# The last 512 value columns of layer 2 as one group, and a last tile closed by column halves, in an fp32 encoder trunk on one core

## The chip, the cores and the metric

The kernel runs on one core of one Trainium2 chip (trn2). The metric is the device time of one execution in microseconds, from runs of the same program; the median of them counts. One execution was also taken by the hardware profiler; the rows quoted in this document come from such executions. Engines are called as in the profile: PE is TensorE with its matmuls, PEld its weight loads, DVE is VectorE, ACT ScalarE, POOL GpSimd and SP SyncE, which issues all DMAs here.

## The reference

The reference is one inference step of a two-layer encoder for 1024 prompt rows and 8 x 16 sample rows, model width 1024, 16 heads of 64 in layer 2, feed-forward width 2816. Layer 1 mixes with sliding-window attention (mixer A); layer 2 with a band of chunks (mixer B), whose keys and values are projected once from the residual stream after layer 1, with a scale and shift of their own. Every sub-layer is closed by

    x <- LN(alpha * x + (1 + gate) * f(x * (1 + scale) + shift))

with LN(x) = (x - mean) * rsqrt(var + 1e-5) * g + b. Cut to what the change touches:

```python
v = (hkv @ w_kv_b[:, 1024:])            # values of layer 2: 1152 rows x 1024 columns
k = (hkv @ w_kv_b[:, :1024])            # keys
q = hm @ w_q_b[0]                       # queries, from hm = x*(1+scale)+shift
s = q k^T * scale + bias, banded; p = softmax(s); o = p v   # each of 16 heads
...
u = causal conv of (h @ w_up); f = (gelu(g) * a) @ w_down   # feed-forward
y = LN(alpha * x + (1 + gate) * f)      # the output, 1152 x 1024
```

All of it is fp32. The kernel's outputs are y, the keys and values and the convolution's state rows.

## The kernel before

The 1152 rows are nine tiles of 128; tile 8 holds the sample rows. Each fp32 operand of a large product is split into a high part (a cast to fp32r) and a low part (the rest, also fp32r), and a product is made of three: low x high, high x low, high x high. So a tile of 128 rows times 1024 rows of weight is 3 x 8 = 24 matmuls into one PSUM bank, whatever the number of columns, up to 512. `wload` (L178) brings a block of weights: a DMA into one of two staging buffers `ws`, a cast on ACT (L165) for `wh`, a subtraction (L176) on POOL or DVE for `wl`. The results go to one of four weight slots, `wslots`, or a place that is given.

The order of each engine's instructions is set by a scheduler that runs over the program in the order it is written, with estimated times; `issue_after` holds some steps back behind others.

The stages of layer 2's mixer, in the order of the program (`attention`, called with l = 1):

- The first quarter of the values, `vproj` (L430): for each token tile in the order 0, 1, 2, 8, 3, 4, 5, 6, 7, `mmX` (L387, matmul L395) multiplies the tile's activations, which lie in `H` (called HX in the trace), by 256 columns; ACT casts the high part from PSUM (L444), DVE subtracts for the low part (L445), and both go out as one DMA to vH (L446). Tiles 4 to 8 are also copied (L450) and stored as outputs.
- Eight chunks of 128 key columns, `kproj` (matmul L383, 384 tokens at a time, three blocks a chunk), with `rescale` on POOL between them.
- The other three quarters of the values, 256 columns each, with two weight slices (512 rows x 256 columns, 24 matmuls a tile together) in slots that rotate.
- Then the slot ring is set to the first two slots, and `qload(0)` loads the first chunk of query weights into slot 0, which the last quarter of the values has used too.
- `load_hm` (L897): for each of the nine tiles a DMA of the residual stream into one of three buffers F (L903), a scale and shift by eight ACT instructions (L907, one for each 128 columns; on DVE at L1006 and L1007 for tile 8), and a split into H: cast (L165) and low part (L176, DVE). A tile of H can be written only when the value projection has read it for the last time.
- Then the attention, head after head: `qblock` (matmuls L383, 24 a block of 384 tokens; drains on ACT at L579 and L590, on DVE at L591), scores (L633 and L636), softmax (DVE L599, ACT L603 with the exponential), transposes (L659), values (L678), sums and normalisation. The projection of the next head's queries is put between the steps of the present one to keep PE full.

At the end of the program stands `down_phase` of layer 2, the feed-forward's second product. Tiles go in groups of three; the last group's last 7 inner steps (the tail) are run tile by tile. `mm` (L1372) makes, for each inner step, three matmuls for each of the two halves of 512 output columns, in two banks. `drain` multiplies by the gate (L1390), `finish` adds the residual and sums (L1401), and `norm_last` (L948) does the LayerNorm: mean (L951), square on ACT (L954), variance (L955), `rsqrt` (L929 to L934). For the very last tile, 8, L961 to L964 then follow each other on DVE, ACT, POOL and DVE, and L965 stores the 128 x 1024 tile.

## Time and profile before

| what | value |
|---|---|
| median of 3 runs | 2803.09 us |
| lowest and highest | 2794.26 and 2809.61 us |
| profiled execution, its own time | 2800.65 us |
| its span, first to last instruction | 2798.5 us |
| mean granted clock of TensorE | 0.988 |
| busy share of the span: PE, PEld | 96%, 86% |
| busy share of the span: DVE, ACT, POOL | 60%, 50%, 38% |
| memory traffic over the span | 165 GB/s |

The own time of the profiled execution lies 2.15 us above its span and 2.44 us below the median. A row of the timeline gives the start, the duration, the engine, the line, the operation, out <- in and the count; what stands in brackets is how long the engine had been idle before it and what it waited for. A row of groups gives the count, then the busy time and the mean nanoseconds of one, then the idle time in front. A row of the chain gives when a piece of the chain that ended last began and how long it held it. Durations of matmuls overlap, since they are pipelined: how far apart two starts are is a better price than a row's duration.

### The profile page before, as it was taken

To read this page: it belongs to the slowest core of one execution; us is meant where nothing else is said; L and a number is where in the kernel's file an instruction comes from. 1 tells how busy PE (TensorE), PEld (TensorE's weight loads), DVE (VectorE), ACT (ScalarE), POOL (GpSimd) and SP (SyncE) were. 2 spreads that over 40 slices of the span, in tenths; PEclk is the share of its full clock that TensorE was granted. 3 is DMA by queue.
4 is the path that set the end of the run, shared out by engine and by line. 5 is a ranking of instruction groups with operands and counts; after the bars stand their busy time and mean duration, and the time that the engine had idled before them with its cause. 6 is when DMAs were issued, how large, how long until landed. Compare 5 with 4: busy or idle time off the path is not lost.

```text
span 2798.5 us, 48858 instructions
## 1 busy us (share of the span) xinstructions
PE 2700.2 (96%) x18086; PEld 2415.9 (86%) x18086; DVE 1665.2 (60%) x3830; ACT 1408.9 (50%) x3012; POOL 1056.7 (38%) x1086
## 2 busy tenths in 40 slices
PE   8999889999999999999999999989899999999998
PEld 5887768999999998888999888867799999998886
DVE  4465757765555566766212677775966555567774
ACT  3465744544444444545425666662555445555441
POOL 1122337676566630001541121141877666640000
PEclk9999999999999999999999999999999999999999
DMA  9655443244444457865975456684222222238661
GB/s 331 193 155 164 124 140 113 97 139 138 155 134 128 146 158 266 310 215 182 303 249 177 113 150 185 168 250 132 99 89 74 78 83 75 76 104 290 232 209 71
DMA packets 215870, 454.47 MB, mean 162 GB/s; under 512 B 39280, under 2 KB 115264, under 8 KB 215632
## 3 DMA queue, kind: packets, MB, share of 16 engines
q1 hardware_dynamic: 215632, 451.35, 50.1%
q8 instruction: 143, 2.34, 0.3%
q14 instruction: 95, 0.78, 0.1%
HBM read 359.40 MB, written 101.30 MB: 165 GB/s over the span
## 4 chain that ended last, share of the span: by engine, by line
PE 77%; DVE 8%; DMA 7%; issue 4%; ACT 3%; POOL 1%; SPq 1%; POOLq 0%; ACTq 0%; DVEq 0%
PE PS L1225 34%; PE PS L1376 17%; PE PS L383 9%; PE PS L395 7%; DMA F<-in_adaw_dram 3%; PE PS L678 2%; PE PS L318 2%; PE PS L659 2%; PE PS L633 1%; DMA ws<-in_wo_dram 1%; DVE F L599 1%; PE PS L636 1%; DVE x1att L176 1%; PE PS L977 1%; PE PS L799 1%
## 5 line engine op out<-in xcount | busy, mean ns | idle before, releaser
L176 POOL TENSOR_TENSOR wl<-ws,wh 128x512 fp32r<-128x512 f32 (+1 forms) x217 | 324.2, 1497 | 649.3 <-ACT wh L165 628.3
L1279 DVE SCALAR_TENSOR_TENSOR PS<-F,PS 128x512 f32<-128x512 f32 (+2 forms) x704 | 349.1, 516 | 143.5 <-ACT PS L1286 63.6
L165 ACT CAST wh<-ws 128x512 fp32r<-128x512 f32 (+1 forms) x321 | 245.2, 769 | 313.6 <-PE PS L1376 99.3
L1225 PE MATMUL PS<-HX,wh 128*128 128x288 f32 x2616 | 401.0, 297 | 0.0
L1225 PEld LDWEIGHTS PS<-HX,wh 128*128 128x128 f32 x2616 | 364.4, 189 | 8.2 <-issue 8.2
L1376 PE MATMUL PS<-wh,HX 128*128 128x512 f32 x1164 | 361.7, 389 | 0.8 <-DVE HX L176 0.8
L1376 PEld LDWEIGHTS PS<-wh,HX 128*128 128x128 f32 x1164 | 218.4, 188 | 46.1 <-DVE HX L176 1.3
L1225 PE MATMUL PS<-HX,wl 128*128 128x288 f32 x1536 | 254.6, 297 | 0.2 <-ACT F L1254 0.2
L383 PE MATMUL PS<-HX,wh 128*128 128x384 f32 x1248 | 245.9, 340 | 0.0
L1376 PE MATMUL PS<-wl,HX 128*128 128x512 f32 x582 | 226.7, 390 | 0.6 <-DVE wl L176 0.6
L1225 PEld LDWEIGHTS PS<-HX,wl 128*128 128x128 f32 x1536 | 220.5, 189 | 7.1 <-issue 5.8
L383 PEld LDWEIGHTS PS<-HX,wh 128*128 128x128 f32 x1248 | 217.3, 189 | 5.4 <-issue 3.1
L1225 PE MATMUL PS<-x1att,wh 128*128 128x288 f32 x1168 | 181.9, 298 | 2.9 <-DVE x1att L176 1.3
L1286 ACT ACTIVATE PS<-F 128x512 f32<-128x512 f32 x176 | 138.1, 785 | 76.3 <-DVE F L1258 64.9
L1225 PEld LDWEIGHTS PS<-x1att,wh 128*128 128x128 f32 x1168 | 163.9, 189 | 8.9 <-issue 4.9
L395 PE MATMUL PS<-wh,HX 128*128 128x256 f32 (+1 forms) x936 | 168.4, 310 | 0.8 <-DVE C L599 0.8
L165 ACT CAST HX<-F 128x384 fp32r<-128x384 f32 (+3 forms) x232 | 136.6, 605 | 62.7 <-PE PS L1376 10.2
L717 POOL TENSOR_TENSOR F<-F,gatt 64x512 f32<-64x512 f32 x62 | 79.5, 1282 | 234.8 <-DVE F L690 181.5
L176 DVE TENSOR_TENSOR HX<-F,HX 128x384 fp32r<-128x384 f32 (+2 forms) x188 | 133.3, 719 | 37.2 <-ACT HX L165 33.6
L1376 PE MATMUL PS<-HX 128*128 128x512 f32 x630 | 145.1, 389 | 0.0
L395 PEld LDWEIGHTS PS<-wh,HX 128*128 128x128 f32 x936 | 133.8, 191 | 10.3 <-issue 1.5
L383 PE MATMUL PS<-HX,wl 128*128 128x384 f32 x624 | 130.3, 348 | 10.1 <-DVE HX L167 4.8
(244 smaller groups left out, 5486.2 us busy)
## 6 DMA issues: line engine op xcount, KB each, us to landing
F<-in_adaw_dram SPq DMA_DIRECT2D x112, 512.0 KB
ws<-in_wup_dram SPq DMA_DIRECT2D x92, 512.0 KB
ws<-in_wdn_dram SPq DMA_DIRECT2D x88, 512.0 KB
actD<-F SPq DMA_DIRECT2D x44, 576.0 KB
F<-actD SPq DMA_DIRECT2D x132, 192.0 KB
F<-in_wdn_dram SPq DMA_DIRECT2D x44, 512.0 KB
x1att<-kH SPq DMA_DIRECT2D x60, 256.0 KB
xd<-F SPq DMA_DIRECT2D x27, 512.0 KB
```

The costliest lines, as they stand in the source:

```text
L165: self.lastact = nc.scalar.copy(out, in_).ins
L176: self.eng(el).tensor_sub(lo, src, hi.bitcast(F32))
L318: mm = nc.tensor.matmul(ps[32 * j : 32 * j + 32, hf * 256 : hf * 256 + 256], self.cT[:, k * 32 : k * 32 + 32], w[n][:, j * 256 : j * 256 + ...
L383: self.nc.tensor.matmul(out, w[a][:, k * 128 : k * 128 + 128], self.Hx(p, k, s0, n), start=i == 0, stop=i == 23)
L395: self.nc.tensor.matmul(out[:, 0:n], H[:, t0 // 128, p, j * kn + k, :], w[a][:, k * n : k * n + n], start=i == 0, stop=i == 23,)
L659: nc.tensor.transpose(t[:, m * 128 : m * 128 + 128], p[:, (kt - k0) * 128 : (kt - k0) * 128 + 128], self.ident)
L678: nc.tensor.matmul(ob[:, i0 * 128 : i0 * 128 + w], vst[a][:, kt, :], pp[:, m1 : m1 + w], start=cnt == 0, stop=cnt == 2 * len(order) - 1, s ...
L717: self.eng("v" if last else "p").tensor_mul(on[r, q], on[r, q], rb[r, :])
L1225: nc.tensor.matmul(out, w[f][a][:, k * 128 : k * 128 + 128], x[:, k, :], start=start and i == 0, stop=i == 11, skip_group_check=True,)
L1279: nc.vector.scalar_tensor_tensor(o, v, w(i), o, op0=ALU.mult, op1=ALU.add)
L1286: nc.scalar.activation(yp, u[:, bl, 2:258], AF.Identity, bias=w(3), scale=w(2))
L1376: nc.tensor.matmul(ps, h[p][:, i * 128 : i * 128 + 128], w[q][:, hf * 512 : hf * 512 + 512], start=j == 0 and k == 0, stop=j == NFF - 1 an ...
```

## The change

It has two parts. The first is in layer 2's value projection. `vproj` takes its weights, the first column and the number of columns as arguments. The second quarter is still 256 columns, but its weights are placed in the buffers of the attention's first head (X1), which are free there. The last two quarters become one group of 512 columns: 24 matmuls of 128 x 512 for each tile, with four weight slices (256 rows x 512 columns) that lie partly in X1 and partly in the last two slots. Its drains have three buffers of their own, and each cast, subtraction, copy and store has 512 columns. Slots 0 and 1 are then not used by the last group, which the ring of query weights takes over.

The second part is `close`, called in place of `mm`, `drain`, `finish` and `norm_last` for the last tile of the output. It runs the 21 tail matmuls of the left 512 columns, then those of the right; each half has its multiplication by the gate (L957 after) and its sum (L958). Then come the mean (L968), the square on ACT (L969), beside it (x + s) * g on DVE (L970), the variance and rsqrt, and for each half x * r + b on DVE (L974) with a store of its own (L975).

The line numbers of the changed kernel lie two higher in the middle of the program: L633 before is L635 after, L907 is L909; in `vproj` L444 is L445 and L450 is L449.

PE's order before, from the end of the value groups to the first scores; L395 is the value projection, L383 the query projection, wl and wh the low and high parts of a weight, `x1att` the buffer of the attention:

```order
L395 MATMUL PS<-wh,HX 128x256 x4
L383 MATMUL PS<-HX,wl 128x384 [waits Pool_49]
L383 MATMUL PS<-HX,wl 128x384 x7
L383 MATMUL PS<-HX,wh 128x384 [waits Activation_49]
L383 MATMUL PS<-HX,wh 128x384 x15
L383 MATMUL PS<-HX,wl 128x384 [waits DVE_49,Activation_49]
L383 MATMUL PS<-HX,wl 128x384 x7
L383 MATMUL PS<-HX,wh 128x384 [waits DVE_49]
L383 MATMUL PS<-HX,wh 128x384 x15
L633 MATMUL PS<-x1att_12291 128x128 [waits DMAHW4_49,DMAHW3_49,DVE_49]
```

After, at the same place:

```order
L395 MATMUL PS<-wh,HX 128x512 x2
L383 MATMUL PS<-HX,wl 128x384 [waits Activation_49]
L383 MATMUL PS<-HX,wl 128x384 x7
L383 MATMUL PS<-HX,wh 128x384 x16
L383 MATMUL PS<-HX,wl 128x384 [waits Activation_49]
L383 MATMUL PS<-HX,wl 128x384 x7
L383 MATMUL PS<-HX,wh 128x384 x16
L383 MATMUL PS<-HX,wl 128x384 [waits Activation_49]
L383 MATMUL PS<-HX,wl 128x384 x7
L383 MATMUL PS<-HX,wh 128x384 [waits DVE_49]
L383 MATMUL PS<-HX,wh 128x384 x15
L635 MATMUL PS<-x1att_12291 128x128 [waits DMAHW7_49,DMAHW0_49,DVE_49]
```

Before, two blocks of queries, 48 products, stand there ahead of the first score; after, three blocks, 72 products; the first of them waits for ACT and no longer for POOL.

ACT's order after, in the first part of the last value group; L445 casts a value tile out of PSUM, L909 scales a tile of hm, and L165 with HX<-F is the cast of a tile of hm into H:

```order
L445 CAST HX<-PS 128x8x64 [waits DMAHW0_49,DMAHW5_49,PE_49,Activation_49]
L165 CAST HX<-F 128x1024
L445 CAST HX<-PS 128x8x64 [waits PE_49]
L165 CAST HX<-F 128x1024
L909 ACTIVATE F<-F,C 128x128 [waits DMAHW0_49,DVE_49]
L909 ACTIVATE F<-F,C 128x128 x7
L445 CAST HX<-PS 128x8x64 [waits DMAHW1_49,PE_49]
L165 CAST HX<-F 128x1024
L909 ACTIVATE F<-F,C 128x128 [waits DMAHW2_49,DVE_49]
L909 ACTIVATE F<-F,C 128x128 x7
L449 COPY F<-PS 128x512 [waits DMAHW6_49,PE_49]
```

The value casts and the refill of H alternate as they did in the last quarter before, now with 512 columns to a cast; the casts of the first two chunks of query weights stand ahead of these rows, where before the first of them stood behind the last value cast.

DVE's last rows after, in the last tile (`x1dn` is the tile's row, C a column of small numbers, ISA the row that multiplies or adds and sums):

```order
L957 TENSOR_TENSOR x1dn_23884<-PS,x1dn_23884 128x512 [waits PE_49]
L958 ISA x1dn_23884,C<-x1dn_23884 128x512 [waits DVE_49]
L958 ISA C 128x1
L968 TENSOR_SCALAR C<-C 128x1 [waits DVE_49]
L970 SCALAR_TENSOR_TENSOR x1dn_23884<-x1dn_23884,C,F 128x1024 [waits DVE_49]
L971 TENSOR_SCALAR C<-C 128x1 [waits Activation_49]
L932 RECIPROCAL C<-C 128x1 [waits Activation_49]
L934 TENSOR_SCALAR C<-C 128x1 [waits DVE_49]
L935 TENSOR_SCALAR C<-C 128x1 [waits DVE_49]
L936 TENSOR_TENSOR C<-C 128x1 [waits DVE_49]
L974 SCALAR_TENSOR_TENSOR x1dn_23884<-x1dn_23884,C,F 128x512 [waits DVE_49]
L974 SCALAR_TENSOR_TENSOR x1dn_23884<-x1dn_23884,C,F 128x512
```

The left half's pair L957 and L958 stands earlier in DVE's queue, between the last small steps of tile 7. Before, two L1390, one L1401 of 1024 columns, the same small steps, L961 and L964 with its wait for POOL stood here.

The diff:

```diff
--- before.py
+++ after.py
@@ -427,27 +427,26 @@
             if n > m:
                 nc.sync.dma_start(self.kS[l][rows, :], t[:, m:n])
 
-    def vproj(self, l, q, banks, tmp):
+    def vproj(self, l, src, c0, n, banks, tmp, dst=None):
         nc = self.nc
-        w = [self.wload(self.I[("wv0", "wv1")[l]][q, i], el="pv"[l == 0]) for i in range(2)]
+        kn = 1024 // n
+        w = [self.wload(src[i], el="vp"[l], dst=dst and dst[i]) for i in range(8 // kn)]
         o0 = (896, 512)[l]
-        cs = slice(q * 256, q * 256 + 256)
+        cs, hs = slice(c0, c0 + n), slice(c0 // 64, (c0 + n) // 64)
         for t in LV:
             ps = self.bank(banks.next())
-            self.mmX(ps, t * 128, w, 4, 256)
+            self.mmX(ps, t * 128, w, kn, n)
             hl, v = tmp.next()
-            v = v[:, 0:256]
+            hl, v = hl[:, 0 : 2 * n], v[:, 0:n]
             ts = slice(t * 128, t * 128 + 128)
             if t < 8:
-                h4 = hl[:, 0:512].rearrange("p (h i d) -> p h i d", i=2, d=64)
-                p3 = ps[:, 0:256].rearrange("p (h d) -> p h d", d=64)
+                h4 = hl.rearrange("p (h i d) -> p h i d", i=2, d=64)
+                p3 = ps[:, 0:n].rearrange("p (h d) -> p h d", d=64)
                 nc.scalar.copy(h4[:, :, 0, :], p3)
                 nc.vector.tensor_sub(h4[:, :, 1, :], p3, h4[:, :, 0, :].bitcast(F32))
-                nc.sync.dma_start(
-                    self.vH[l][ts, 4 * q : 4 * q + 4, :], hl[:, 0:512].bitcast(F32).rearrange("p (h d) -> p h d", d=128)
-                )
+                nc.sync.dma_start(self.vH[l][ts, hs, :], hl.bitcast(F32).rearrange("p (h d) -> p h d", d=128))
             if t * 128 >= o0:
-                nc.scalar.copy(v, ps[:, 0:256])
+                nc.scalar.copy(v, ps[:, 0:n])
                 nc.sync.dma_start(self.O[("va", "vb")[l]][t * 128 - o0 : t * 128 - o0 + 128, cs], v)
             if t == 8:
                 nc.sync.dma_start(self.vS[l][:, cs], v)
@@ -524,7 +523,7 @@
         with ExitStack() as es:
             if l == 0:
                 es.enter_context(self.tc.issue_after(self.lastx))
-            self.vproj(l, 0, kvb, kvt)
+            self.vproj(l, I[("wv0", "wv1")[l]][0], 0, 256, kvb, kvt)
         if l == 0:
             self.skew(0)
         else:
@@ -533,8 +532,11 @@
                 self.kproj(1, c, self.wload(I["wk1"][c]), kvb, kvt)
                 self.rescale(c, zr)
             self.rescale(8, zr)
-            for q in range(1, 4):
-                self.vproj(1, q, kvb, kvt)
+            vt = [(self.X2[:, i * 1024 : i * 1024 + 1024], self.F[:, i * 512 : i * 512 + 512]) for i in range(3)]
+            spare = [tuple(self.X1[:, o + i : o + i + 1024] for i in (0, 1024)) for o in (0, 2048, 5120, 7168)]
+            spare += [self.wslots[2], (self.wslots[3][0], self.X1[:, 4096:5120])]
+            self.vproj(1, I["wv1"][1], 256, 256, kvb, kvt, spare[0:2])
+            self.vproj(1, I["wv1h"], 512, 512, kvb, Ring(vt), spare[2:6])
             self.wring = Ring(self.wslots[0:2])
             qload(0)
             self.load_hm(Ring([pall[:, i * 1024 : i * 1024 + 1024] for i in range(3)]), self.affine(4, (8, 9), 1))
@@ -944,6 +946,33 @@
         nc.vector.tensor_scalar_add(v, mv[:, 1:2], EPS)
         self.rsqrt(r, v)
         return mv[:, 0:1], r
+
+    def close(self, t, row, x, ydst, product, junk):
+        nc = self.nc
+        part, rr = self.sm.next(), self.sm.next()
+        s, v, r = part[:, 0:1], rr[:, 0:1], rr[:, 1:2]
+        halves = [slice(hf * 512, hf * 512 + 512) for hf in range(2)]
+        for hf, n in enumerate(halves):
+            ps = product(hf)
+            nc.vector.tensor_mul(row[:, n], ps, self.gateS[:, n])
+            nc.vector.tensor_tensor_reduce(
+                out=row[:, n],
+                in0=row[:, n],
+                in1=x[:, n],
+                scale=1.0,
+                scalar=0.0,
+                op0=ALU.add,
+                op1=ALU.add,
+                accum_out=part[:, hf : hf + 1],
+            )
+        nc.vector.tensor_scalar(s, s, part[:, 1:2], -1.0 / D, op0=ALU.add, op1=ALU.mult)
+        nc.scalar.activation(junk, row, AF.Square, bias=s, accum_out=v)
+        nc.vector.scalar_tensor_tensor(x, row, s, self.lng, op0=ALU.add, op1=ALU.mult)
+        nc.vector.tensor_scalar(v, v, 1.0 / D, EPS, op0=ALU.mult, op1=ALU.add)
+        self.rsqrt(r, v)
+        for n in halves:
+            nc.vector.scalar_tensor_tensor(x[:, n], x[:, n], r, self.lnb[:, n], op0=ALU.mult, op1=ALU.add)
+            nc.sync.dma_start(ydst[t * 128 : t * 128 + 128, n], x[:, n])
 
     def norm_last(self, t, x, s, ydst, junk):
 
@@ -1369,8 +1398,8 @@
         todo = []
         aff = None
 
-        def mm(w, h, t, i, j):
-            for hf in range(2):
+        def mm(w, h, t, i, j, hs=(0, 1)):
+            for hf in hs:
                 ps = self.bank(2 * i + hf)
                 for k, (p, q) in enumerate(((1, 0), (0, 1), (0, 0))):
                     nc.tensor.matmul(
@@ -1452,9 +1481,18 @@
                     finish(*todo.pop(0))
             wh = [load(g, j) for j in range(NFF - nt, NFF)]
             for i, t in enumerate(ts):
+                row = rows.next()
+                if last and final and i == 2:
+
+                    def product(hf):
+                        for k, (w, h) in enumerate(wh):
+                            mm(w, h, t, i, NFF - nt + k, (hf,))
+                        return self.bank(2 * i + hf)
+
+                    self.close(t, row, xs[i], xdst, product, tmp)
+                    continue
                 for k, (w, h) in enumerate(wh):
                     mm(w, h, t, i, NFF - nt + k)
-                row = rows.next()
                 drain(i, t, row)
                 if final:
                     finish(t, row, xs[i])
@@ -1576,7 +1614,8 @@
     z["wv0"] = quarters(w[:, D + 256 :])
     z["wo0"] = halves(g["w_o_a"][0].reshape(16, 64, D)[ho].reshape(D, D))
     z["wk1"] = cols(g["w_kv_b"][:, :D])
-    z["wv1"] = quarters(g["w_kv_b"][:, D:])
+    z["wv1"] = quarters(g["w_kv_b"][:, D : D + 512])
+    z["wv1h"] = halves(g["w_kv_b"][:, D:])[1]
     z["wq1"] = cols(g["w_q_b"][0])
     z["wo1"] = halves(g["w_o_b"][0])
     z["wup"] = np.stack([cols(g["w_up"][l]) for l in range(2)])
```

## The prediction

> **What bounds the kernel now.** The page comes first: its span, its busy line, and the shares of the chain that ended last.
>
> ```profile
> span 2798.5 us, 48858 instructions
> PE 2700.2 (96%) x18086; PEld 2415.9 (86%) x18086; DVE 1665.2 (60%) x3830; ACT 1408.9 (50%) x3012; POOL 1056.7 (38%) x1086
> PE 77%; DVE 8%; DMA 7%; issue 4%; ACT 3%; POOL 1%; SPq 1%; POOLq 0%; ACTq 0%; DVEq 0%
> ```
>
> TensorE (PE) is busy for 96% of the span and is 77% of the chain. An edit can gain in three ways: fewer or cheaper products, a hole in PE's work closed, or work after PE's last product shortened. This edit touches all three, so I read the windows view next, in stretches cut at the places of the edit. The columns are: window, length, busy microseconds (count) of PE, weight load, DVE, ACT and POOL, the granted clock, the DMA share, GB/s.
>
> ```profile
> 1475.00:1501.00 26.00, 26.00 (x220) 26.00 (x218) 3.41 (x8) 5.70 (x14) 4.76 (x2) 1.00 0.45 154
> 1501.00:1527.10 26.10, 26.08 (x218) 25.87 (x216) 8.22 (x12) 19.63 (x48) 0.00 (x0) 1.00 0.60 200
> 1527.10:1558.20 31.10, 22.82 (x108) 21.33 (x108) 20.61 (x46) 20.73 (x42) 8.20 (x3) 0.84 0.40 128
> 1558.00:1600.00 42.00, 40.94 (x275) 37.64 (x273) 28.09 (x88) 26.54 (x65) 6.80 (x8) 1.00 0.49 126
> 1750.00:1800.00 50.00, 49.72 (x405) 43.74 (x404) 37.04 (x124) 31.87 (x82) 6.83 (x9) 1.00 0.76 202
> ```
>
> The two value groups shown (the last is the second row) are full, and so are the two stretches of attention at the end. Between them lie 31.10 us in which PE does 108 products and is granted 0.84 of its clock. PE's own timeline shows that hole (start, duration, engine, line, shapes, count; in brackets the idle time before and what ended it).
>
> ```profile
> 1526.44 0.64 PE L395 MATMUL PS<-wh,HX 128*128 128x256 f32 x4
> 1530.96 2.93 PE L383 MATMUL PS<-HX,wl 128*128 128x384 f32 x8 [3.88 <-POOL wl L176]
> 1533.68 3.12 PE L383 MATMUL PS<-HX,wh 128*128 128x384 f32 x16
> 1544.86 0.47 PE L633 MATMUL PS<-x1att 128*128 128x128 f32 x1 [3.89 <-DVE x1att L591]
> 1547.00 2.76 PE L383 MATMUL PS<-HX,wl 128*128 128x384 f32 x8
> 1558.19 1.64 PE L383 MATMUL PS<-HX,wl 128*128 128x384 f32 x8
> ...
> 1527.44 1.04 ACT L165 CAST wh<-ws 128x1024 fp32r<-128x1024 f32 x1
> 1528.55 2.35 POOL L176 TENSOR_TENSOR wl<-ws,wh 128x1024 fp32r<-128x1024 f32 x1 [48.78 <-ACT wh L165]
> ```
>
> The first query weights go into the slot that the last value group reads. ACT can cast them only once that group's last product has ended (1526.44 + 0.64 = 1527.08), POOL makes their low part after that, and PE starts at 1530.96. Eight products then take 2.93 us where eight take 1.64 us at 1558.19. The second hole, 3.89 us, waits for the query drain L591 on DVE, behind the refill of H (tiles of hm, L897 to L915), which also could start only as the last group passed each tile.
>
> **Streaming.** The change replaces 432 products of 256 columns by 216 of 512. Prices are groups of the chain of waits (start, microseconds held, count).
>
> ```profile
> 1360.93 88.40 PE PS L383 x510
> 1449.33 59.00 PE PS L395 x492
> 2519.86 203.85 PE PS L1376 x898
> ```
>
> A 256-column product holds 59.00/492 = 0.1199 us, one of 512 columns 203.85/898 = 0.2270, one of 384 columns 88.40/510 = 0.1733. So 432 x 0.1199 = 51.8 us becomes 216 x 0.2270 = 49.0: **-2.8 us**, and the groups end at about 1524.3. The slope is (0.2270 - 0.1199)/256 = 0.418 ns a column, which leaves 119.9 - 107.0 = 12.9 ns for each product whatever its width. The bounds: 0 if the weight load sets the pace, and -5.5, twice the saving. [...]
>
> **The start of attention.** The 108 products of that stretch are 72 of L383 (72 x 0.1733 = 12.5) and 36 short ones. For a short one I estimate 0.14 us, between 49.72/405 = 0.123 and 40.94/275 = 0.149 of the two attention windows: 5.0. So 17.5 us of work took 31.1, and 13.6 are lost. In the order after, the first two weight chunks of the queries go into slots that the last value group does not read, so their casts stand before that group's drains, and the wait for POOL goes with its 3.88 us. What is late next is the third block of query products, which reads the last tiles of H. The last group now lasts 9 x 24 x 0.2270 = 49 us in place of 9 x 24 x 0.1199 = 26, so the refill starts 23 us sooner ahead of its end. Its prices (group rows: count | busy, mean ns | idle before):
>
> ```profile
> L907 ACT ACTIVATE F<-F,C 128x128 f32<-128x128 f32 x40 | 16.2, 487 | 2.6 <-DMA F<-hmD 2.6
> L176 DVE TENSOR_TENSOR HX<-F,HX 128x1024 fp32r<-128x1024 f32 x9 | 14.1, 1574 | 5.8 <-ACT HX L165 5.8
> L165 ACT CAST HX<-F 128x1024 fp32r<-128x1024 f32 x9 | 9.4, 1051 | 0.1
> L664 ACT CAST HX<-PS 128x512 fp32r<-128x512 f32 x1 | 0.6, 588 | 0.0
> ```
>
> The last loads of hm stand in the chain of waits; this one held 6.73 us.
>
> ```profile
> 1533.15 6.73 DMA F<-hmD
> ```
>
> ACT has, inside the last group, five tiles' scaling (40 L907 hold 16.2 us), nine casts (9.4), eight 512-column value casts (8 x 0.588 = 4.7) and five copies at the same price (2.9): 33 of 49 us, so it keeps up. After the group's end stay one value cast, two casts of H and about 1.57 + 1.57 us of DVE: some 3.9 us, while the third block's first product comes 48 x 0.1733 = 8.3 us after the end. So all 72 run without a hole, 12.5 us. Then PE runs out: the next product of L383 waits for a bank that ACT and DVE free, behind what stands ahead on ACT, of which these are the rows.
>
> ```profile
> 1546.93 1.28 ACT L603 ACT_TABLE_LOAD   x1
> 1548.22 0.40 ACT L603 ACTIVATE F<-F,C 128x128 f32<-128x128 f32 x1
> 1550.70 0.51 ACT L603 ACTIVATE F<-F,C 128x256 f32<-128x256 f32 x1 [1.98 <-DVE C L599]
> 1553.61 0.56 ACT L579 ACTIVATE F<-PS 64x128 f32<-64x128 f32 x2 [1.46 <-PE PS L383]
> 1554.18 0.38 ACT L590 ACTIVATE x1att<-PS 64x256 fp32r<-64x256 f32 x1
> 1554.46 1.03 ACT L165 CAST wh<-ws 128x1024 fp32r<-128x1024 f32 x1
> 1554.80 0.42 DVE L591 SCALAR_TENSOR_TENSOR x1att<-PS,x1att 64x256 fp32r<-64x256 f32 x1
> 1556.39 0.19 ACT L603 ACTIVATION_READ_ACCUMULATOR F<-F,C 128x1 f32 x1
> ```
>
> After: 0.56 + 0.38 + 1.03 + 1.28 + (0.40 + 0.19) + (0.51 + 0.19) + 0.38 + 0.42 = 5.3, with the hand-overs 5.5 us, partly filled by short products. The second chunk's products start at 1524.3 + 12.5 + 5.5 = 1542.3 in place of 1558.19, 15.9 earlier. But by the order 95 products then stand ahead of them, not 108; the 13 others come later (13 x 0.15 = 2.0). Net 13.9 earlier, 2.8 of which is streaming: **-11.1 us**. Bounds: the whole 13.6, and the 3.88 of the POOL wait alone. PE is 97% to 99% busy in the windows after that, so I let the head start stand.
>
> **The tail.** DVE's timeline behind the last products:
>
> ```profile
> 2784.26 1.37 DVE L1390 TENSOR_TENSOR x1dn<-PS,x1dn 128x512 f32<-128x512 f32 x2 [1.89 <-PE PS L1376]
> 2785.66 1.23 DVE L1401 CUSTOM_DVE_ANT_0 x1dn<-x1dn 128x1024 f32<-128x1024 f32 x1
> 2786.93 0.15 DVE L951 TENSOR_SCALAR C<-C 128x1 f32<-128x1 f32 x1
> 2789.76 0.16 DVE L961 TENSOR_TENSOR C<-C 128x1 f32<-128x1 f32 x1
> 2793.71 1.23 DVE L964 TENSOR_TENSOR x1dn<-x1dn,F 128x1024 f32<-128x1024 f32 x1 [3.79 <-POOL x1dn L963]
> ```
>
> And the stores of the output as issued (of the row only the time of the last issue counts, 2795.0), with a store of 256 KB (a value tile of layer 1) from the chain:
>
> ```profile
> L965 SPq DMA_DIRECT2D out_y_dram<-x1dn x9: 332/338/338, 2628.9 to 2795.0; - x9
> ...
> 72.05 2.97 DMA vH<-HX
> ```
>
> The first half's drain now lies beside the second half's 21 products (21 x 0.2270 = 4.8 us against two DVE steps of 512 columns at 1.37/2 = 0.69 each, behind other rows of tile 7). Behind the last product stand one multiply and one sum of 512, 0.69 + 0.69, where a multiply of 512 and a sum of 1024 stood, 0.69 + 1.23: -0.54, and +0.12 for a small step more (as L951). The big saving is at the end: from 2789.76 to 2793.71 + 1.23 = 2794.94 L961, L962, L963 and L964 follow each other; after, two L974 of 512 columns (0.69 each) follow the rsqrt, so the last DVE row ends near 2789.76 - 0.42 + 1.38 = 2790.7: -4.2. The last store, 256 KB in place of 512 KB, is priced by the 2.97 us of a 256 KB store early in the kernel against 2798.5 - 2795.0 = 3.5: -0.5. Sum **-4.7 us**, between -4.2 (store at no gain) and -5.2. The 1024-column L970 lies beside ACT's square and costs nothing; without that cover it would cost 1.23.
>
> **Sum.** -2.8 - 11.1 - 4.7 = -18.6. The profiled execution took 2800.65 us (span 2798.5 and 2.15 around it), so 2782.05; it lies 2.44 below the median 2803.09, from which the sum gives 2784.5. I say **2783**.
>
> **Rivals.**
> 1. The refill of H still comes last: only the POOL wait goes, because the hm loads (6.73 us) start late in SP's queue. For it: the second hole ended on L591, behind that refill. Against: 23 us more room. -2.8 - 3.9 - 4.7 = -11.4: about 2790, no change.
> 2. The head start is given back: attention waits for its k and v loads, which now come after the value groups, or the output projection waits for weights that come when they did. For it: DMA share 0.76 at 1750:1800. Against: PE there is 99% busy. -2.8 - 4.7 = -7.5: 2794, no change.
> 3. A cold clock after the new gap. The first eight products after 3.88 us idle took 2.93 us, not 8 x 0.1733 = 1.39, and the next sixteen 3.12 us, not 2.77, at a granted 0.84; the wait for ACT of up to 5.5 us falls between short products and could do the same: 1.5 to 4 us back, 2787. [...]
> 4. Slower: the refill starves the last value group. ACT works in order, and a scaling step that waits for its hm load holds the value casts queued behind it, thus PE's banks. Three buffers make two more turns of load + 8 us (scaling 3.2, cast 1.05, low part 1.57, queueing). At 6.73 us a load that is 2 x 14.7 = 29 of 49 us. It starts to count from 16.5 us a load; at 33 us it adds 2 x 41 - 49 = 33, and -18.6 + 33 gives 2815 to 2818. Against: 33 us is five times the row, at a DMA share of 0.60.
>
> That the change does not do what it says is not open: the order shows the merged products, the early weights and the split tail.
>
> **How the numbers follow.** 0.5% of 2803.09, 14 us, is about what a measurement of this kernel can tell from no change; the line to "faster" is 2789.1. Forecast 0.66, of which 0.58 lies below the line and 0.08 above, since a sum of -18.6 stands only 4.6 us beyond it; rival 1 0.12, rival 2 0.12, rival 3 0.06 (still faster), rival 4 0.04. Faster 0.58 + 0.06 = 0.64, same 0.08 + 0.24 = 0.32, slower 0.04. The forecast's own range: at best -5.5 - 13.6 - 5.2 = -24.3, 2776, less about 2 us for the parts of the order that moved with no reason: 2774. The upper end takes in rivals 1 and 2: 2794. Rival 4 and the rest are left out.
>
> **What would show it right or wrong.** Right: 216 L395 rows near 0.227 us; no wait for POOL at the first L383; the 72 products in one piece of about 12.5 us at a clock near 1.00; the second chunk's L383 about 14 us earlier; no L962 to L964 in the last tile; the last store's start 4 us nearer the last product. Wrong: idle time of PE in the last value group ended by ACT or by hmD loads (rival 4); a third block that waits for DVE's low part (rival 1); a first up-projection that begins as late as before (rival 2); a PE clock under 0.9 in the stretch (rival 3).

## The result and the profile after

The changed kernel takes 2784.98 us in the median of 6 runs (2779.85 to 2788.8) where the kernel before takes 2801.62: a ratio of 0.9933, with an interval from 0.9913 to 0.9953. Two later sets of runs of it, on two different chips, gave 0.9949 (0.9938 to 0.9961) and 0.9958 (0.9945 to 0.9971). So it is faster by 0.4 to 0.7%, 12 to 19 us.

The page of the execution that was profiled (2788.8 us by its own time, the slowest of its six):

```profile
span 2786.9 us, 48360 instructions
PE 2693.8 (97%) x17870; PEld 2399.5 (86%) x17870; DVE 1664.8 (60%) x3825; ACT 1406.6 (50%) x2998; POOL 1051.2 (38%) x1085
PE 82%; DVE 7%; DMA 6%; ACT 2%; issue 1%; POOL 1%; SPq 1%; DVEq 0%; POOLq 0%; ACTq 0%
```

PE has 216 products fewer and its share of the chain rose from 77% to 82%: holes went. The windows of the last two value groups and of the start of attention show them filled (columns as in the prediction):

```profile
1450.26:1475.46 25.20, 25.20 (x217) 25.20 (x217) 3.40 (x8) 6.75 (x15) 4.80 (x2) 1.00 0.63 191
1475.46:1525.68 50.22, 50.22 (x218) 40.55 (x217) 16.20 (x28) 29.02 (x60) 0.00 (x0) 1.00 0.67 215
1525.68:1543.65 17.97, 16.54 (x97) 15.57 (x95) 9.73 (x26) 10.01 (x19) 2.36 (x1) 1.00 0.47 146
```

The second row is the group of 512 columns: 50.22/216 = 0.2325 us a product. The third holds the 72 query products and the short ones up to the second chunk. The granted clock is 1.00 in all three rows; at the start of attention it was 0.84 before. Here is that third row as PE's timeline, with the two rows of ACT and DVE that end the refill of H:

```profile
1525.68 1.58 PE L383 MATMUL PS<-HX,wl 128*128 128x384 f32 x8
1527.10 2.93 PE L383 MATMUL PS<-HX,wh 128*128 128x384 f32 x16
1534.03 1.55 PE L383 MATMUL PS<-HX,wl 128*128 128x384 f32 x8
1538.19 0.22 PE L635 MATMUL PS<-x1att 128*128 128x128 f32 x1
1540.64 0.42 PE L635 MATMUL PS<-x1att 128*128 128x320 f32 x1 [0.43 <-DVE C L601]
1542.20 0.33 PE L661 MATMUL PS<-C,F 128*128 128x128 f32 x1 [1.00 <-ACT F L605]
1543.65 1.63 PE L383 MATMUL PS<-HX,wl 128*128 128x384 f32 x8
...
1526.37 2.00 ACT L165 CAST HX<-F 128x1024 fp32r<-128x1024 f32 x2
1527.45 2.36 DVE L176 TENSOR_TENSOR HX<-F,HX 128x1024 fp32r<-128x1024 f32 x2 [0.26 <-ACT HX L165]
```

The first query product follows the last value product with no wait; the 72 take 1538.19 - 1525.68 = 12.5 us; the refill ends at 1529.81, 4.1 us after the group; the second chunk starts 18.0 us after it. Before, the refill ended with this row, at 1547.90, 20.8 us after its last group (1527.08):

```profile
1546.67 1.23 DVE L176 TENSOR_TENSOR HX<-F,HX 128x1024 fp32r<-128x1024 f32 x1
```

The end of the program, from PE's last product on:

```profile
2777.62 0.39 PE L1405 MATMUL PS<-wh,HX 128*128 128x512 f32 x1
2778.05 0.69 DVE L957 TENSOR_TENSOR x1dn<-PS,x1dn 128x512 f32<-128x512 f32 x1 [1.63 <-PE PS L1405]
2778.77 0.69 DVE L958 CUSTOM_DVE_ANT_0 x1dn<-x1dn 128x512 f32<-128x512 f32 x1
2779.75 1.28 DVE L970 SCALAR_TENSOR_TENSOR x1dn<-x1dn,C,F 128x1024 f32<-128x1024 f32 x1
2779.81 1.15 ACT L969 ACTIVATE x1dn<-x1dn,C 128x1024 f32<-128x1024 f32 x1 [7.38 <-DVE C L968]
2782.40 1.41 DVE L974 SCALAR_TENSOR_TENSOR x1dn<-x1dn,C,F 128x512 f32<-128x512 f32 x2
2783.18 0.99 SPq L975 DMA_DIRECT2D out_y_dram<-x1dn  x2
```

Before, PE's last product was this one:

```profile
2784.51 0.39 PE L1376 MATMUL PS<-wh,HX 128*128 128x512 f32 x1
```

From the last product's start to the end of the span stand 2786.9 - 2777.62 = 9.3 us, where before stand 2798.5 - 2784.51 = 14.0. DVE's 1.28 us at L970 lie beside ACT's square.

**Where the time came from.** The same place in two programs can be compared by PE's starts. I call "lead" how much earlier than in the profile of before a product starts, less the same difference at the last product of layer 1, which lies ahead of all that is changed (profiles differ there already, by 4.2 us earlier to 3.5 later, also for one and the same kernel). Microseconds of lead, from the traces of this study:

| kernel, profile | 2nd query chunk | last query product | last score | first of the feed-forward | 200 products on | last product |
|---|---|---|---|---|---|---|
| changed, 1st | 15.6 | 12.8 | 8.6 | 10.6 | 8.0 | 8.0 |
| changed, 2nd (e0_again) | 15.5 | 12.6 | 9.0 | 10.9 | 8.3 | 8.5 |
| changed, 3rd (e10_after) | 15.4 | 12.5 | 13.3 | 13.1 | 11.0 | 10.8 |
| groups only (e1_groups) | 15.2 | 12.3 | 12.7 | 12.8 | 11.2 | 11.4 |
| groups only, 2nd (e7_groups_again) | 15.4 | 12.6 | 10.3 | 11.8 | 9.0 | 9.0 |
| end only (e2_close) | -0.3 | -0.4 | 0.1 | 0.1 | -0.2 | -0.1 |
| late weights (e3_reuse) | 8.0 | 2.0 | 1.4 | 1.5 | -0.1 | 0.1 |
| late weights, refill free (e11_reuse_free) | 11.1 | 8.3 | 7.2 | 8.4 | 4.6 | 4.7 |
| two groups of 256 (e4_256early) | 6.3 | 5.7 | 7.7 | 5.8 | 5.7 | 5.7 |
| two groups of 512 (e8_two512) | 20.2 | 17.6 | 17.1 | 18.6 | 16.0 | 15.7 |
| hm loaded three times (e9_refill3) | -7.5 | -13.5 | -14.7 | -13.8 | -16.5 | -16.4 |
| changed, fewer loads (e5_after_noload) | 15.4 | 12.6 | 13.6 | 9.0 | 6.7 | 6.9 |
| before, fewer loads (e6_before_noload) | 0.1 | 0.1 | -0.2 | -0.9 | -3.3 | -3.2 |

For the first profile the sum closes: a lead of 8.0, 4.7 at the end, and 1.1 us lost ahead of the change give 11.6 = 2798.5 - 2786.9. All rows are measured against one single profile of before; `e2_close`, which has its value groups, agrees with it within 0.4 us.

### The profile page after: what moved, and what is told of

Read it like the earlier page. It is cut to its first block, busy times and chain, and to the rows that moved or that the text cites. A ratio compares the mean times of both kernels' runs of the same rounds, so it can differ in the third digit from the quotient of the medians.

```text
span 2786.9 us, 48360 instructions
## 1 busy us (share of the span) xinstructions
PE 2693.8 (97%) x17870; PEld 2399.5 (86%) x17870; DVE 1664.8 (60%) x3825; ACT 1406.6 (50%) x2998; POOL 1051.2 (38%) x1085
## 3 DMA queue, kind: packets, MB, share of 16 engines
q8 instruction: 141, 2.31, 0.3%
## 4 chain that ended last, share of the span: by engine, by line
PE 82%; DVE 7%; DMA 6%; ACT 2%; issue 1%; POOL 1%; SPq 1%; DVEq 0%; POOLq 0%; ACTq 0%
PE PS L1254 34%; PE PS L1405 19%; PE PS L383 11%; PE PS L395 8%; DMA F<-in_adaw_dram 2%; PE PS L680 2%; PE PS L318 2%; PE PS L661 2%; PE PS L635 1%; DMA ws<-in_wo_dram 1%; PE PS L638 1%; DVE F L601 1%; DVE x1att L176 1%; PE PS L801 1%; PE PS L1006 1%
## 5 line engine op out<-in xcount | busy, mean ns | idle before, releaser
L176 POOL TENSOR_TENSOR wl<-ws,wh 128x512 fp32r<-128x512 f32 (+1 forms) x212 | 310.6, 1468 | 638.1 <-ACT wh L165 605.3
L165 ACT CAST wh<-ws 128x512 fp32r<-128x512 f32 (+1 forms) x317 | 240.9, 765 | 317.5 <-PE PS L1405 103.6
L1405 PEld LDWEIGHTS PS<-wh,HX 128*128 128x128 f32 x1164 | 218.4, 188 | 46.3 <-DVE HX L176 1.3
L383 PE MATMUL PS<-HX,wh 128*128 128x384 f32 x1248 | 245.7, 339 | 0.0
L383 PEld LDWEIGHTS PS<-HX,wh 128*128 128x128 f32 x1248 | 216.9, 189 | 5.4 <-issue 2.7
L395 PE MATMUL PS<-x1att,HX 128*128 128x512 f32 (+1 forms) x846 | 189.0, 369 | 3.3 <-ACT x1att L165 2.2
L395 PEld LDWEIGHTS PS<-x1att,HX 128*128 128x128 f32 x846 | 142.5, 188 | 31.9 <-ACT x1att L165 2.9
L165 ACT CAST HX<-F 128x384 fp32r<-128x384 f32 (+3 forms) x232 | 136.4, 605 | 65.0 <-PE PS L1405 10.5
L1405 PEld LDWEIGHTS PS<-HX 128*128 128x128 f32 x630 | 118.2, 188 | 24.6
```

What stands on the lines that cost most here:

```text
L165: self.lastact = nc.scalar.copy(out, in_).ins
L176: self.eng(el).tensor_sub(lo, src, hi.bitcast(F32))
L383: self.nc.tensor.matmul(out, w[a][:, k * 128 : k * 128 + 128], self.Hx(p, k, s0, n), start=i == 0, stop=i == 23)
L395: self.nc.tensor.matmul(out[:, 0:n], H[:, t0 // 128, p, j * kn + k, :], w[a][:, k * n : k * n + n], start=i == 0, stop=i == 23,)
L1405: nc.tensor.matmul(ps, h[p][:, i * 128 : i * 128 + 128], w[q][:, hf * 512 : hf * 512 + 512], start=j == 0 and k == 0, stop=j == NFF - 1 an ...
```

## The experiments

The theory is the prediction's: shorter streaming, early query weights with a refill of H that has room, a shorter end. Its rivals are that one of the two parts carries all, and that the head start is given back. A figure "under before" is what the ratio makes of the median of before in the same set of runs.

**The two parts alone.** `e1_groups` has the value groups and the old end of the last tile:

```diff
-                if last and final and i == 2:
-                    ...
-                    self.close(t, row, xs[i], xdst, product, tmp)
-                    continue
```

> The value groups of the change alone; the last tile is closed as before. My account: -2.8 - 11.1 = -13.9 under before, or -9 to -10 if the loss in the attention's last heads belongs to the order; last product to end 14.0 us as before. Rival, the head start is given back and the gain came from the tail: -3 to -5.

Measured: 0.9956 (0.9943 to 0.9968), 12.3 us under before. `e2_close` has the old `vproj` and its old calls, and `close`:

> The new end of the last tile alone; value groups as before. My account: -4.7 us, and the profile shows 9.3 us from the last product's start to the end of the span where before has 14.0; PE's holes at the start of attention as before (3.9 us for POOL, 3.9 us for DVE). If the first half's drain were not hidden beside the second half's products, the last product itself would come 1.4 us later and the gain were about -3.3.

Measured: 0.9980 (0.9967 to 0.9993), 5.6 us under before. Its last rows:

```profile
2784.54 0.39 PE L1403 MATMUL PS<-wh,HX 128*128 128x512 f32 x1
2789.32 1.41 DVE L972 SCALAR_TENSOR_TENSOR x1dn<-x1dn,C,F 128x512 f32<-128x512 f32 x2
```

The last product starts where it did before (2784.51), so the first half's drain is hidden, and the span ends at 2793.7, 9.2 us later. Both parts gain, each about what it was given; that the groups' gain comes from the tail is out.

**Early weights.** `e3_reuse` puts two of the four weight slices of the 512-column group into the slots that the query weights take over:

```diff
-            spare += [self.wslots[2], (self.wslots[3][0], self.X1[:, 4096:5120])]
+            spare += self.wslots[0:2]
```

> The changed kernel, but two of the four weight slices of the 512-column group lie in slots 0 and 1, which the query weights take over, as the last quarter's did before. It keeps the long last group, the 512-column products and the tail. My account: the wait of 3.9 us for POOL at the first query product comes back, with up to 2 us of slower clock; the second hole (for the query drain behind the refill of H) does not: 4 to 6 us slower than the changed kernel, some -12 to -14 under before. Rival, the early weights carry the whole gain at the start of attention: 11 us slower than the changed kernel, about -7.5 under before. Rival, they carry nothing since the refill hides it: no slower than the changed kernel.

Measured: 0.9977 (0.9965 to 0.9990), 6.4 us under before, about 8 us of the gain gone (14.3 us under in the set of runs beside it). The expectation failed: the wait for POOL came back as foreseen, but so did the refill of H, and the time is near the one that the first rival gave, -7.5, by which the early weights carry the whole gain there. Timelines of the four engines at that place (the group ends at 1524.64 - 2.33 = 1522.3):

```profile
1521.04 1.05 ACT L165 CAST wh<-ws 128x1024 fp32r<-128x1024 f32 x1 [2.31 <-PE PS L395]
1522.00 2.93 ACT L165 CAST HX<-F 128x1024 fp32r<-128x1024 f32 x3
1522.24 2.35 POOL L176 TENSOR_TENSOR wl<-ws,wh 128x1024 fp32r<-128x1024 f32 x1 [86.25 <-ACT wh L165]
1524.64 2.06 PE L383 MATMUL PS<-HX,wl 128*128 128x384 f32 x8 [2.33 <-POOL wl L176]
1526.50 4.15 PE L383 MATMUL PS<-HX,wh 128*128 128x384 f32 x16
1538.23 1.22 DVE L176 TENSOR_TENSOR HX<-F,HX 128x1024 fp32r<-128x1024 f32 x1
```

ACT casts three tiles of H in one piece, right behind the query weights, though it had stood idle for 2.31 us before; the refill ends at 1539.45, 17 us after the group, long as the group was. The cause stands in `load_hm`: the splits of tiles 4 to 8 are issued behind `lead`, the last ACT copy ahead of them in the program, and that is the query weights' cast. A weight that waits for the group's end holds the refill back with it. To test that, `e11_reuse_free` is the same kernel without the rule:

```diff
-            with ExitStack() as es:
-                if t >= 4:
-                    es.enter_context(self.tc.issue_after(lead))
-                self.split(s3, self.H[:, t, 0], self.H[:, t, 1], "a", "v")
+            self.split(s3, self.H[:, t, 0], self.H[:, t, 1], "a", "v")
```

> The run with two weight slices in slots 0 and 1 again, without the rule in load_hm that issues the splits of tiles 4 to 8 behind the first query weights' cast (issue_after). The query weights still wait for the end of the last value group. New theory: in that run the refill of H stopped at tile 3 because its casts stood behind the query weights' cast, so late weights cost more than the wait for POOL. Then here the refill ends some 4 to 6 us after the group's end instead of 17.7, the 2 to 4 us for POOL and some slow clock stay, the second query chunk comes 10 to 11 us earlier than before (7.9 there, 15.5 in the changed kernel), and the time is 9 to 13 under before. If the casts' place does not matter, nothing changes against that run: 6 under before.

Measured: 0.9963 (0.9949 to 0.9976), 10.4 us under before, and these rows (its group ends at 1523.0):

```profile
1524.57 5.62 DVE L176 TENSOR_TENSOR HX<-F,HX 128x1024 fp32r<-128x1024 f32 x2 [0.26 <-ACT HX L165]
1525.86 2.45 PE L383 MATMUL PS<-HX,wl 128*128 128x384 f32 x8 [2.88 <-POOL wl L176]
1528.10 3.75 PE L383 MATMUL PS<-HX,wh 128*128 128x384 f32 x16
```

The refill ends at 1530.19, 7.2 us after the group (4 to 6 were expected; two DVE rows took 5.62 us in place of 2.36), the wait for POOL stays, and the lead at the second chunk is 11.1 as the new theory had it. So the early weights are worth two things: the wait itself, with the slow clock behind it (0.93 from 1525 to 1550, where the changed kernel has 1.00; 15.6 - 11.1 = 4.5 us), and the freed refill (11.1 - 8.0 = 3.1 us there, and more further on). By time alone the two kernels can't be told apart, since their intervals overlap; it is the traces that show the difference.

**The length of the last group.** `e4_256early` keeps early weights and makes two groups of 256 columns:

```diff
-            self.vproj(1, I["wv1h"], 512, 512, kvb, Ring(vt), spare[2:6])
+            for q in (2, 3):
+                self.vproj(1, I["wv1"][q], 256 * q, 256, kvb, kvt, spare[2 * q - 2 : 2 * q])
```

> The changed kernel, but the last 512 value columns again as two groups of 256 with drains as before; their weights stay off slots 0 and 1, so the first query weights are ready early. It keeps the new tail. My account: no wait for POOL at the first query product, but the last group lasts 26 us again, so the refill of H ends some 20 us after it as before and the second hole comes back longer (about 8 us for the query drain behind the refill): the second chunk's products at most 4 us earlier than before, total 5 to 9 us under before. Rival, the early weights carry the gain and the group's length nothing: within 3 us of the changed kernel.

Measured: 0.9954 (0.9941 to 0.9966), 12.9 us under before: more than expected, and by time not to be told from the changed kernel. The trace shows what was foreseen at the start of attention, in a smaller size (the group ends at 1527.4):

```profile
1540.90 0.48 PE L635 MATMUL PS<-x1att 128*128 128x128 f32 x1 [4.97 <-DVE x1att L593]
1541.39 2.93 PE L383 MATMUL PS<-HX,wl 128*128 128x384 f32 x8
1542.93 1.22 DVE L176 TENSOR_TENSOR HX<-F,HX 128x1024 fp32r<-128x1024 f32 x1
```

The refill ends at 1544.15, 16.7 us after the group; PE waits 4.97 us, and its next eight products of 384 columns take 2.93 us, where eight took 1.55 at 1527.44; the granted clock from 1527.4 to 1553.9 is 0.87. The lead at the second chunk is 6.3, against 15.6 with the long group. But 5.7 of the 6.3 are left at the end, where the changed kernel keeps 8.0 to 10.8 of 15.5. So in these profiles the long group gives 9 us where it stands and 2 to 5 at the end, and no run shows the latter by time. A part of what this kernel gains is probably streaming of its own: its first two groups have their weights in X1, and by the changed kernel's price for that (0.1167 us a product against 0.1200, see the price of a product below) 432 x 0.0033 = 1.4 us is my estimate of it.

**What the refill costs.** `e9_refill3` makes each load of hm three times:

```diff
             nc.sync.dma_start(s, self.hmD[t])
+            nc.sync.dma_start(s, self.hmD[t])
+            nc.sync.dma_start(s, self.hmD[t])
```

> The changed kernel with each load of hm made three times, one after the other into the same buffer. The fourth rival of the prediction put the point from which the refill starves the last value group at 16.5 us a load, with 2 x (load + 8) us against 49. One load held 6.7 us, three of them some 10 to 18. My account: no or little hole inside the last value group, the third block of query products waits a few us for the refill, 0 to 5 us slower than the changed kernel. If the group's length were no cover (the finding of the run with two groups of 256, that it hardly matters), the refill would end some 12 us later and so would the attention: 8 us or more slower.

Measured: 1.0029 (1.0017 to 1.0042), 20 us slower than the changed kernel beside it, far more than expected. Timelines of SP, ACT and PE in that kernel (L905 to L907 are the three loads):

```profile
1486.13 0.33 SPq L905 DMA_DIRECT2D F<-hmD  x1
1493.22 0.32 SPq L906 DMA_DIRECT2D F<-hmD  x1
1497.48 0.32 SPq L907 DMA_DIRECT2D F<-hmD  x1
...
1513.95 0.32 SPq L907 DMA_DIRECT2D F<-hmD  x1
...
1517.45 0.32 SPq L905 DMA_DIRECT2D F<-hmD  x1
...
1501.63 3.20 ACT L911 ACTIVATE F<-F,C 128x128 f32<-128x128 f32 x8 [5.62 <-DMA F<-hmD]
...
1535.56 2.10 PE L383 MATMUL PS<-HX,wl 128*128 128x384 f32 x8 [3.50 <-ACT F L449]
1547.90 0.47 PE L635 MATMUL PS<-x1att 128*128 128x128 f32 x1 [6.29 <-DVE x1att L593]
```

The three loads of the first buffer take 15.5 us (1486.13 to 1501.63), below the 16.5 of the formula. But the next turn starts only at 1517.45, 31 us after the first and not 23: by these starts a repeated load waits for the one before it (1486.13, 1493.22, 1497.48), and the loads of the other two buffers, the last at 1513.95, stand ahead of the next turn in SP's order. The value group itself is not starved: it takes 50.2 us as before. What waits is what comes behind it, 3.50 and 6.29 us in these rows. The fourth rival's mechanism is real: ACT's copy of the value tile whose products end at 1499.80 starts only at 1504.73, behind the scaling of 1501.63 that had waited 5.62 us for its load. Its place was wrong, and its price left SP's queue out.

**Is the head start given back to the loads?** `e0_again` and `e10_after` are the changed kernel, unedited, and `e7_groups_again` is the groups alone.

> The changed kernel once more, nothing edited, for a second profile and more runs. My account (streaming -2.8, start of attention -11.1, tail -4.7): 14 to 20 us under the kernel before, the second query chunk's products some 12 to 14 us earlier than before, last product to end 9.3 us. The first profile of it lost 4 of its 12 us head start between 1820 and 1890 us, in the attention's last heads. If that belongs to the new order of instructions, this profile shows the same loss at the same place; if it is chance of one execution, the head start there differs by 2 us or more from the first profile.

> The value groups alone once more, for a second profile: its first one kept the whole head start through the attention's last heads (13.1 of 12.8 us), with the same order of instructions in which two profiles of the changed kernel lost 4 us. If that was chance, this profile loses 1 us or more there and the times of the two builds of it lie as far apart as those of the changed kernel; if it belongs to the build, it keeps the head start again, and its time lies within 2 us of the changed kernel's.

> The changed kernel a third time, beside the two runs above on the same chip, and for a third profile. 14 to 18 us under before. The head start at the second query chunk is 15.6 us against before in both profiles so far; 8.0 and 8.6 of it were left at the end of the feed-forward part. If the loss belongs to the order of instructions, this profile ends with 8 to 9 again; if it is chance, with 10 or more.

Measured: 0.9949, 0.9952 (0.9941 to 0.9964) and 0.9958. Between the last query product and the last score these five profiles lost 4.2, 3.6, -0.8, -0.4 and 2.3 us. The second repeated the first, as it would if the loss belonged to the new order of instructions; but the third profile of the same kernel did not, and PE's 490 products of that stretch stand in the same order in all five and in before. So the loss differs from one execution to the next; what makes it differ is not shown. In the first profile 2.0 of the 4.2 are back at the first product of the feed-forward. The windows of that stretch, for before, the first profile and the third:

```profile
1815.40:1884.70 69.30, 57.51 (x494) 43.56 (x492) 49.72 (x175) 49.02 (x118) 28.94 (x20) 0.95 0.86 252
```

```profile
1803.60:1877.50 73.90, 60.28 (x502) 45.62 (x500) 51.03 (x180) 49.69 (x118) 31.01 (x20) 0.93 0.82 236
```

```profile
1804.80:1873.50 68.70, 58.16 (x494) 44.14 (x492) 49.70 (x175) 49.24 (x118) 29.53 (x20) 0.95 0.89 254
```

PE is busy for 82 to 85% there and the DMA engines for 82 to 89%, so loads were the suspects. `e5_after_noload` and `e6_before_noload` leave out 8 MB of them, half of the cached keys and values, in the changed kernel and in the one before:

```diff
-                nc.sync.dma_start(k3[:, :, 0:P0], I["ckB"][s, :, 4 * p : 4 * p + 4, :])
+                if p == 0:
+                    nc.sync.dma_start(k3[:, :, 0:P0], I["ckB"][s, :, 0:4, :])
...
-                nc.sync.dma_start(v3, I["cvB"][s, :, 512 * p : 512 * p + 512].rearrange(...))
+                if p == 0:
+                    nc.sync.dma_start(v3, I["cvB"][s, :, 0:512].rearrange(...))
```

> The changed kernel without the loads of cached keys and values for the last eight sample items (8 x 1 MB in the attention's last 60 us; those items use what the first eight left in the buffers). If the head start is given back there because the loads of that stretch set its pace, the head start at the last score row is within 1 us of that at the last query product, and the ratio to the partner kernel without the same loads is the full -16 to -18 us. If it is given back by the order of instructions on the engines, 3 to 4 us are still lost there.

> The kernel before without the same loads (keys and values of the last eight sample items), the partner of the run above. Faster than before by what the loads cost in that stretch: 3 to 8 us if they set its pace, nothing if they are hidden.

Measured: 0.9967 (0.9955 to 0.9978) and 1.0018 (1.0003 to 1.0033), both against the full kernel before. Neither got faster than its partner with the loads, and their ratio, 0.9967/1.0018 = 0.9949, is the changed kernel's own. The scheduler also put the last part of attention in another order without them, on all engines, and that may cost what the missing loads give. So the loads are not shown to set the pace there, and not quite excluded either. In the fewer-loads pair the changed kernel's lead over its partner is 15.3 us at the second chunk and 10.1 at the end: given back in part again, this time behind the last score.

The other loss stands between the feed-forward's first product and its 200th: 1.6 to 2.8 us in the five profiles, 2.6 with two groups of 512. The schedule of those first steps differs from before in all of these kernels, in the same rows. `e2_close` and `e4_256early` have the old order there and lose 0.3 and 0.1 us. `e6_before_noload` has the new one, with before's value groups and no lead at all, and loses 2.4. So it goes with the order and not with the head start. Here are 30 us from near that stretch's first product (2009.5 and 2000.0) in before and in the changed kernel:

```profile
2010.00:2040.00 30.00, 23.85 (x158) 22.45 (x157) 27.63 (x40) 15.77 (x41) 19.81 (x18) 0.89 0.21 70
```

```profile
2002.00:2032.00 30.00, 20.72 (x134) 18.91 (x133) 26.79 (x39) 15.39 (x40) 19.20 (x19) 0.89 0.20 71
```

PE gets 24 products fewer done. No run changed that order alone.

**A version that beats both.** `e8_two512` makes the first 512 value columns one group too; its weights lie in the four slots, and the first two key chunks' weights in the attention's first-head buffers:

```diff
-            self.vproj(l, I[("wv0", "wv1")[l]][0], 0, 256, kvb, kvt)
+            if l == 0:
+                self.vproj(0, I["wv0"][0], 0, 256, kvb, kvt)
+            else:
+                self.vproj(1, I["wv1"][0], 0, 512, kvb, Ring(vt))
...
-                self.kproj(1, c, self.wload(I["wk1"][c]), kvb, kvt)
+                self.kproj(1, c, self.wload(I["wk1"][c], dst=spare[c] if c < 2 else None), kvb, kvt)
...
-            self.vproj(1, I["wv1"][1], 256, 256, kvb, kvt, spare[0:2])
```

> The changed kernel with the first 512 value columns as one group of 512-column products too, ahead of the keys (its weights in the four slots; the first two key chunks' weights in the attention's first-head buffers). By the two widths as the changed kernel's trace has them, two groups of 256 hold 25.9 + 25.2 us and one of 512 holds 50.2: -0.9 us, and -2.8 by the prediction's prices. If the merged products were what carries the change, doubling them would bring some -10 more. If only the early weights and the refill's room matter: within 3 us of the changed kernel.

Measured: 0.9930 (0.9916 to 0.9944), beside 0.9958 (0.9945 to 0.9971) for the changed kernel on the same chip: 6 us faster by the medians (2781.81 and 2788.02), more than the 3 expected. Its windows, from early in layer 2's first value group to the end of the last:

```profile
1320.00:1370.00 50.00, 50.00 (x234) 41.48 (x234) 25.55 (x49) 24.95 (x53) 22.31 (x13) 1.00 0.71 258
1370.00:1471.30 101.30, 101.30 (x584) 101.02 (x583) 13.19 (x25) 29.53 (x56) 62.12 (x31) 1.00 0.86 282
1471.30:1521.70 50.40, 50.40 (x219) 40.72 (x218) 16.26 (x28) 30.30 (x61) 2.41 (x1) 1.00 0.58 201
```

The changed kernel has 41.10 us of PE in the 43.00 us from 1320 on, here PE is full: at the change of layers the changed kernel waits 0.77, 0.48 and 0.66 us, twice ahead of the transposes that make H (L1006 there), and `e8_two512` does not wait, which brings about 1.9 us of the 4.6 us of lead that it has more at the first query product (10.9 against 6.3). Most of the rest is streaming, some 2 us by the prices that follow. Merged products as such do not bring 10 us.

**The price of a product.** The chain of waits of `e8_two512` holds two prices for the same shape of 128 x 512:

```profile
1346.08 25.66 PE PS L395 x113
1471.61 50.22 PE PS L395 x216
```

The first row is most of the group whose weights lie in the four slots: 25.66/113 = 0.2271 us a product. In the second, 50.22/216 = 0.2325, more than half of the products read weights that lie in X1. With 256 columns it is the other way round: from start to start 0.1200 us in before, with the weights in the slots, and 25.20/216 = 0.1167 in the changed kernel, with the weights in X1. So in these rows the price of a product goes with the buffer that holds its weights. But in the second group of `e8_two512` the twelve products of a tile that read X1 take 2.80 us (1510.50 to 1513.30), 0.2333 each, and the twelve behind them, ten of which read slots, 2.78, 0.2317 each and not 0.2271: the buffer may not be all of it, and no run shows the reason.

## Why the prediction was right, point by point

The first median lies 2 us off the forecast of 2783 and inside the range, and each of the three terms can be seen in the traces. That it lies so close is in part luck: the terms give 18.6 us, the three sets of runs 18.8, 14.3 and 11.8, and the leads at the end, with the 4.7 of the shorter end, 12.7 in the first profile and 15.5 in the third. One step failed, the head start that was let stand.

- **Streaming**, -2.8: the three groups behind the keys took 648 x 0.1200 = 77.8 us before and 75.4 after (1450.26 to 1525.68): -2.3. The parts were off in two directions. The 512-column product holds 0.2325 us and not 0.2270, so the merged group gains 51.8 - 50.2 = 1.6; and the 256-column group ahead of it got shorter by 216 x (0.1200 - 0.1167) = 0.7, a gain that the prediction did not have. Both go with the move of the weights into X1, to which the prediction gave no price. Two products of 256 less one of 512 are 2 x 0.1200 - 0.2271 = 0.013 us with the weights in the slots, as the prediction's 12.9 ns has it, and 2 x 0.1167 - 0.2325 = 0.001 with X1. The rows here give no single fixed cost of a product.
- **The start of attention**, 15.9 us earlier at the second chunk: 15.6, with 12.5 us for the 72 products and 18.0 from group to second chunk, both as worked out. The refill ended 4.1 us after the group (3.9 forecast; the prediction's own rows, one after the other, give 0.59 + 1.05 + 1.57 + 1.57 = 4.8, but DVE's low parts took 1.18 us each and not 1.57). Net of the products that moved, -13.9 was forecast; the lead at the last query product is 12.8.
- **The reason given for it was incomplete.** The prediction put the earlier refill down to the group's length alone. `e3_reuse` and `e11_reuse_free` show that it also needs the early weights, through the issue rule in `load_hm`. `e4_256early` shows the other side: with early weights and a last group of 256 columns the refill ends 16.7 us after the group. The number came out because the change does both.
- **"PE is 97% to 99% busy in the windows after that, so I let the head start stand"**: the step that failed. Those windows end at 1800. In the 69 us from 1815.4 on PE of before is busy for 57.51 of 69.30, and at the feed-forward's start for 23.85 of 30. Of 12.3 to 12.8 us, 8.0 to 11.4 were left at the end in five profiles: the last heads took between -0.8 and 4.2, differently in each execution, and the new order at the feed-forward's start 1.6 to 2.8. The prediction had seen the latter in the order and gave it about 2 us of the range, toward a gain. What the time shows agrees: the groups alone gained 12.3 us where the prediction's terms give 13.9, the whole 12 to 19 where they give 18.6.
- **The end**, -4.7: 14.0 us to 9.3, term by term: DVE's last row ends 6.19 us behind the last product's start and not 10.43, the rest is the smaller store.
- **Rivals.** The refill does not come last; the clock stayed at 1.00 at the start of attention (1525.68 to 1543.65); the head start was given back in part (the second rival), but no run shows the loads as the reason, and at most 0.2 us of it went between the last score and the feed-forward, where the output projection with its weights stands. The fourth rival took each load made three times (15.5 us for the first buffer, where one load held 6.73), and then struck behind the group (3.50 and 6.29 us), not in it.

Of the three ratios of the changed kernel one lies within 0.5% of before and one at that bound: the head start that did not stand takes the change from clear to borderline, as the prediction's case of "no change" had it.

## What to carry to other kernels

Of a head start of 12.3 to 12.8 us, 8.0 to 11.4 were left at the end of this kernel: read the windows up to the end of the program, not just the ones next to the edit. When a wait goes, look for what the program itself ties to the waiting instruction (an issue rule, a place in an engine's queue), since that may be worth much: here the wait was worth 4.5 us at the second chunk and the refill tied to it 3.1. Put the weights of what follows into buffers that the product ahead does not use, and give a product that stands ahead of a refill more length; here the two together did it (a lead of 15.6 us at the second chunk, 8.0 with late weights, 6.3 with a short last group), and what the length alone is worth at the end was seen in single profiles and not in the times. And when weights move to another buffer, read the price of their products again: for 512 columns it was 0.2271 us here and 0.2325.

## What the runs showed of the hardware

Slow products stood behind waits shorter than the 3.88 us of the prediction: after 2.33 us idle (`e3_reuse`) eight products of 384 columns took 2.06 us and the next sixteen 4.15, where the changed kernel has 1.58 and 2.93, and the granted clock from 1521.5 to 1547.66 was 0.93; after 2.88 us (`e11_reuse_free`) they took 2.45 and 3.75, at 0.93 from 1525 to 1550. A product's price was not one number for one shape: for 512 columns it was 0.2271 us with the weights in the slots and 0.2325 with most of them in X1, for 256 columns 0.1200 with the weights in the slots and 0.1167 in X1. And the same program, profiled again, reaches the end of layer 1 earlier or later by microseconds (1.1, 3.5 and 2.0 us behind before for the changed kernel; 2.1 and -4.2 for the groups alone, 6.3 apart), which is more than some of the terms that one wants to read from a single profile.
